# A hybrid decoder layer on Trainium2: 22,680 unread products of constants ahead of the first conditioning product

## The chip, the cores and the metric

The kernel runs on one core of one Trainium2 chip. The metric is the device time of one execution in microseconds, of the slowest (here the only) core. Times on TensorE, VectorE, ScalarE, GpSimd and SyncE are those of a hardware profile of one execution, in which these engines are called PE (with PEld for its weight loads), DVE, ACT, POOL and SP.

## What is computed

One layer of a decoder with 256 prompt tokens and 8 x 4 sample tokens (288 rows in all), model width 2,048. The conditioning product is the first matrix product; its results scale and shift everything that follows.

```python
def _layer(x, c, conv_prefix, chunk, g_mix, g_ffn, w_ada, b_ada, w_in, w_conv, g_v, w_sg, b_sg,
           w_pa, w_pb, w_out, w_ffn_in, w_ffn_out):
    n, s, _ = x.shape
    mod = (jax.nn.silu(c) @ w_ada + b_ada).reshape(n, N_MOD, 1, D_MODEL)
    sh_m, sc_m, gt_m, sh_f, sc_f, gt_f = [mod[:, i] for i in range(N_MOD)]
    h = _rms(x, g_mix) * (1 + sc_m) + sh_m
    proj = h @ w_in
    ...
    z = c_gate * hc
    conv = sum(w_conv[k] * zfull[:, k:k + s] for k in range(CONV_WIDTH))
    ya = b_gate * conv
    ...
    yb = u * sp.reshape(n, s, SG_DIM)
    merged = jax.nn.sigmoid(ga) * (ya @ w_pa) + jax.nn.sigmoid(gb) * (yb @ w_pb)
    x = x + gt_m * (merged @ w_out)
    h2 = _rms(x, g_ffn) * (1 + sc_f) + sh_f
    gate, up = jnp.split(h2 @ w_ffn_in, 2, axis=-1)
    x = x + gt_f * ((jax.nn.silu(gate) * up) @ w_ffn_out)
    ...
```

## The kernel before

All activations are held transposed, as 16 tiles of 128 features by 288 tokens. A weight matrix is streamed from HBM in blocks of at most 128 x 2,048 fp32 numbers into seven buffers (tag `raw`, `RAW = 7`). ScalarE casts 512 columns of a block to fp32r (`hi`, L448) and VectorE makes the rest (`lo`, L454, L243); the activations are split in the same way. A product of a 128x128 weight slice and a 128x288 activation tile is then a triple of three fp32r matmuls (L224, L227, L229): `hi` weight by `hi` activation, `hi` by `lo`, `lo` by `hi`. All weight slices start at a multiple of 128 elements in their buffer and all activation tiles at the start of theirs. In the first stages and in one later block the tile has ten columns more (`TU` = 298).

The conditioning product (class `Ada`, L388) is different: plain fp32, the 32 conditioning columns as the stationary operand, the weight block as the moving one, four 32-column strips at a time. Its units a0 and a1 (two blocks each) come first, and their results are needed for the first two tiles of the normalised input.

TensorE's instructions run in the order in which they are written. At the start that order is 24 bf16 matmuls of a tile of ones (`warm`, L571, into the PSUM tile `idle`), then a0's first block, five more such matmuls, a0's second block, and the first input tiles. For the start the orders of ScalarE, VectorE and SyncE are written by hand as well (a manual schedule that begins ahead of the first `load`). SyncE's queue issues the loads: a0, the first piece of w0, one x tile, the rest of w0, a1, another x tile, wK, wA and so on, each waiting until its buffer among the seven is free. The tile of ones `wb` is written by GpSimd.

The change touches only the function that writes this order (`_body`): it adds a nested function and one call of it, between the definitions and the list of steps, so its instructions stand ahead of the first `warm(24)` on TensorE.

```python
    wb = const("wb", [P, 288], BF16)
    G.memset(wb, 1.0)
    idle = psmain()
    ...
    steps = [Do(lambda: warm(24)), a0[0], Do(lambda: warm(5)), a0[1]]
    ...
    for s in stream[:2]:
        s.load()
    w0.load(0, 512)
    load_x(0)
    w0.load(512)
    for s in a1:
        s.load()
```

Of the kernel before, what the change touches and what calls it, by code (L numbers as in the profile page):

```python
# [8 lines left out]
F32 = mybir.dt.float32  # L9
F32R = mybir.dt.float32r  # L10
# [4 lines left out]
P = 128  # L15
D = 2048
T = 288
# [7 lines left out]
RAW = 7  # L25
# [59 lines left out]
def decoder_kernel(tc, d):  # L85
    nc = tc.nc
    from contextlib import ExitStack

    with ExitStack() as es:
        def pool(name, bufs=1, **kw):  # L90
            return es.enter_context(tc.tile_pool(name=name, bufs=bufs, **kw))

        pc = pool("const")
        pw = pool("wstream")
        pslot = pool("slots", SLOTS)
        ptmp = pool("tmp", 5)
        pps = pool("psum", 4, space=bass.MemoryType.PSUM)
        with tc.manual_schedule(engines={nc.tensor.engine}):
            _body(tc, nc, d, pc, pw, pslot, ptmp, pps)


def _body(tc, nc, d, pc, pw, pslot, ptmp, pps):
    ids = [0]

    def nm(s):
        ids[0] += 1
        return f"{s}_{ids[0]}"

    def const(name, shape, dt=F32):
        return pc.tile(shape, dt, tag=name, name=name)  # L110
# [7 lines left out]
    def psmain():  # L118
        return pps.tile([P, 512], F32, tag="main", name=nm("pm"), bufs=4)
# [4 lines left out]
    V, A, G, PE, SY = nc.vector, nc.scalar, nc.gpsimd, nc.tensor, nc.sync  # L124
# [227 lines left out]
    class Step:  # L352
        defer = False
        raw = None
# [209 lines left out]
# [3 lines that stand above are left out]
# [475 lines left out]
        tail.close()  # L1042


    rh1 = h1.__getitem__
    def at(main, plan):
        out, n = [], 0
        for s in main:
            out.append(s)
            if isinstance(s, Blk):  # L1050
                n += 1
                out += plan.pop(n, [])
        assert not plan
        return out
# [101 lines left out]
    for s in steps:  # L1156
# [11 lines left out]
        i = pos[id(s)]  # L1168
# [124 lines left out]
```

## Time and profile before

| | us |
|---|---|
| median of 2 runs (1624.91 to 1625.12) | 1625.01 |
| the profiled execution | 1625.02 |
| its span, first to last instruction | 1623.2 |
| TensorE busy with matmuls | 1613.2 |
| VectorE busy | 1015.8 |
| ScalarE busy | 736.2 |
| mean DMA rate over the span | 220 GB/s |

The time lies 1.8 us above the span: it holds what is around the first and the last instruction. Busy times add the durations of single instructions where they do not overlap; matmuls do overlap, so a matmul's own duration is longer than the distance to the next one's start. A row of the timeline shows start, duration, engine, line, operation, the tile written and the tiles read, and how many alike follow each other in it. In the table by windows the number in brackets counts the instructions that were active in the window.

In the first 40 us the DMA engines move some 400 GB/s, and the first conditioning product starts at 6.29 us.

### The profile page before, as it was taken

To read this page: it belongs to the slowest core of one execution; us is meant where nothing else is said; L and a number is where in the kernel's file an instruction comes from. 1 tells how busy PE (TensorE), PEld (TensorE's weight loads), DVE (VectorE), ACT (ScalarE), POOL (GpSimd) and SP (SyncE) were. 2 spreads that over 40 slices of the span, in tenths; PEclk is the share of its full clock that TensorE was granted. 3 is DMA by queue.
4 is the path that set the end of the run, shared out by engine and by line. 5 is a ranking of instruction groups with operands and counts; after the bars stand their busy time and mean duration, and the time that the engine had idled before them with its cause. 6 is when DMAs were issued, how large, how long until landed. Compare 5 with 4: busy or idle time off the path is not lost.

```text
span 1623.2 us, 31599 instructions
## 1 busy us (share of the span) xinstructions
PE 1613.2 (99%) x12645; PEld 1549.3 (95%) x12645; DVE 1015.8 (63%) x2196; ACT 736.2 (45%) x1358; POOL 21.8 (1%) x66
## 2 busy tenths in 40 slices
PE   9999999999999999999999999999999999999997
PEld 8998999999999999999999999999999999999997
DVE  6676788877755567667744555555555555555565
ACT  5533344643444334456633444444444444444454
POOL 0000000000000000011000000000000000000000
PEclk9999999999999999999999999999999999999999
DMA  9887866777877666654576556453464434645341
GB/s 376 324 318 286 313 238 212 273 284 289 298 292 309 261 260 228 241 178 158 185 307 263 207 180 209 156 173 110 164 229 157 168 121 161 225 157 172 110 161 59
DMA packets 59140, 357.60 MB, mean 220 GB/s; under 512 B 6736, under 2 KB 9840, under 8 KB 28272
## 3 DMA queue, kind: packets, MB, share of 16 engines
q1 hardware_dynamic: 58704, 355.45, 60.0%
q8 instruction: 99, 1.62, 0.4%
q14 instruction: 49, 0.40, 0.1%
q10 hardware_dynamic: 288, 0.13, 0.0%
HBM read 352.46 MB, written 3.09 MB: 219 GB/s over the span
## 4 chain that ended last, share of the span: by engine, by line
PE 98%; DMA 1%; DVE 0%; DVEq 0%; ACT 0%; issue 0%; ACTq 0%
PE pm L224 31%; PE pm L227 31%; PE pm L229 30%; PE ada L388 5%; DMA raw<-in_wK 1%; DMA raw<-in_w 0%; DVE st L1023 0%; DMA ct<-in_c 0%; PE px L227 0%; PE px L818 0%; PE px L224 0%; PE px L229 0%; PE px L859 0%; PE px L198 0%; PE px L860 0%; PE px L861 0%
## 5 line engine op out<-in xcount | busy, mean ns | idle before, releaser
L224 PE MATMUL pm<-s,hi 128*128 128x288 f32 (+1 forms) x3750 | 1108.9, 296 | 0.0
L227 PE MATMUL pm<-s,hi 128*128 128x288 f32 (+1 forms) x3750 | 1105.0, 295 | 0.0
L229 PE MATMUL pm<-s,lo 128*128 128x288 f32 (+1 forms) x3738 | 1101.3, 295 | 0.0
L448 ACT CAST hi<-raw 128x512 fp32r<-128x512 f32 (+1 forms) x963 | 587.4, 612 | 812.0 <-PE pm L227 776.7
L454 DVE TENSOR_TENSOR lo<-raw,hi 128x512 fp32r<-128x512 f32 (+1 forms) x849 | 577.2, 681 | 439.2 <-ACT hi L448 426.8
L224 PEld LDWEIGHTS pm<-s,hi 128*128 128x128 f32 x3750 | 705.1, 188 | 15.2 <-issue 13.3
L227 PEld LDWEIGHTS pm<-s,hi 128*128 128x128 f32 x3750 | 704.7, 188 | 0.0
L229 PEld LDWEIGHTS pm<-s,lo 128*128 128x128 f32 x3738 | 702.7, 188 | 0.0
L243 DVE TENSOR_TENSOR lo<-raw,hi 128x512 fp32r<-128x512 f32 x111 | 74.7, 676 | 29.6 <-ACT hi L448 28.9
L388 PE MATMUL ada<-raw,cs 128*32 128x512 f32 (+2 forms) x1152 | 88.3, 452 | 0.0
L388 PEld LDWEIGHTS ada<-raw,cs 128*32 128x32 f32 x1152 | 30.9, 110 | 44.7 <-issue 42.0
L766 DVE TENSOR_TENSOR s<-pm,s 128x288 f32<-128x288 f32 x72 | 32.9, 457 | 19.8 <-PE pm L229 19.8
L298 DVE TENSOR_TENSOR s<-t,s 128x288 fp32r<-128x288 f32 (+1 forms) x76 | 34.6, 459 | 6.4 <-ACT s L296 6.4
L296 ACT CAST s<-t 128x288 fp32r<-128x288 f32 (+1 forms) x76 | 32.5, 433 | 12.9 <-DVE t L798 12.4
L338 DVE SCALAR_TENSOR_TENSOR x<-pm,mod,x 128x256 f32<-128x256 f32 x79 | 37.5, 475 | 0.0
L944 DVE SCALAR_TENSOR_TENSOR t<-t,pm 128x288 f32<-128x288 f32 x42 | 19.1, 454 | 20.6 <-PE pm L229 20.6
L758 DVE TENSOR_TENSOR s<-pm,s 128x288 f32<-128x288 f32 x48 | 21.8, 454 | 10.4 <-PE pm L229 9.5
L337 DVE TENSOR_TENSOR t<-pm,mod 128x32 f32<-128x32 f32 x79 | 15.2, 192 | 18.5 <-PE pm L229 18.5
L743 DVE SCALAR_TENSOR_TENSOR s<-pm,s 128x256 f32<-128x256 f32 x48 | 23.1, 480 | 4.1 <-PE pm L229 4.1
L749 DVE TENSOR_TENSOR s<-s,rb 128x288 f32<-128x288 f32 x48 | 21.5, 449 | 0.0
L172 ACT ACTIVATE t<-x 128x288 f32<-128x288 f32 x29 | 12.9, 445 | 17.4 <-DVE x L341 17.4
L177 DVE TENSOR_TENSOR acc<-acc,t 128x288 f32<-128x288 f32 x33 | 15.0, 456 | 8.2 <-ACT t L172 8.2
(158 smaller groups left out, 479.7 us busy)
## 6 DMA issues: line engine op xcount, KB each, us to landing
raw<-in_fi SPq DMA_DIRECT2D x84, 1024.0 KB, 4.9
raw<-in_a SPq DMA_DIRECT2D x64, 1024.0 KB, 8.8
raw<-in_f SPq DMA_DIRECT2D x64, 704.0 KB, 4.0
raw<-in_wD SPq DMA_DIRECT2D x34, 1024.0 KB, 5.7
raw<-in_aE SPq DMA_DIRECT2D x16, 1024.0 KB, 10.3
raw<-in_wo SPq DMA_DIRECT2D x16, 1024.0 KB, 6.4
raw<-in_wC SPq DMA_DIRECT2D x19, 768.0 KB, 5.7
raw<-in_pa SPq DMA_DIRECT2D x8, 1024.0 KB, 5.9
```

Of the source, the lines that this page charges most:

```text
L224: PE.matmul(out, wh, ah, start=first, stop=False)
L227: end_ = PE.matmul(out, wh, al, start=False, stop=turn and last)
L229: end_ = PE.matmul(out, wl, ah, start=False, stop=last)
L243: lows.pop(0)[1]()
L296: A.copy(hi, a)
L298: V.tensor_tensor(lo, a, hi.bitcast(F32), ALU.subtract)
L338: V.scalar_tensor_tensor(x[:, m, :TP], ps[:, :TP], mod[:, gt0 + m, 0:1], x[:, m, :TP], ALU.mult, ALU.add)
L388: PE.matmul(acc[32 * j : 32 * j + 32, :w], cs[:, kt, :], self.raw[:, o : o + w], start=kt == 0, stop=kt == 15, tile_position=(0, 32 * j), ...
L448: A.copy(hi, self.raw[:, s * 128 : e * 128])
L454: sub()
L743: V.scalar_tensor_tensor(t[:, :TP], ps[:, :TP], t[:, T : T + 1], t[:, :TP], ALU.add, ALU.add)
L766: V.tensor_tensor(a, ps[:, :T], a, ALU.add)
```

## The change

A function `bench` is added and called once. VectorE fills a 128x2,048 tile with 0.75 and casts it to an fp32r tile; ScalarE casts it to two more. These four tiles take four of the seven stream buffers. TensorE runs 48 bf16 matmuls on `wb`, then walks a list of 1,260 combinations (s, a, b, l) of start places. For each of them it runs six triples: weight slices of the first tile start at i x 128 + s, moving operands of the third tile at s + a and 512 + s + b, and weight slices of the second tile at i x 128 + s + l, all in elements of four bytes. The first 320 entries have s = 0, five fixed values of a = b, and l from 0 to 63; the next 400 are drawn at random with a = b; the last 540 are drawn freely. All products go to the PSUM tile `idle`, each one with both start and stop set, and nothing reads it.

```diff
+    def bench():
+        import random
+
+        f = pw.tile([P, 2048], F32, tag="raw", name=nm("bench"), bufs=RAW)
+        V.memset(f, 0.75)
+        rs = []
+        for i in range(3):
+            r = pw.tile([P, 2048], F32R, tag="raw", name=nm("benchr"), bufs=RAW)
+            A.copy(r, f) if i else V.tensor_copy(r, f)
+            rs.append(r)
+        r0, r1, r2 = rs
+        def mm(s, m):
+            PE.matmul(idle[:, :T], s, m, start=True, stop=True)
+
+        def w(r, k, s=0):
+            return r[:, P * (k % 12) + s : P * (k % 12) + s + P]
+
+        def mv(r, o):
+            return r[:, o : o + T]
+
+        for i in range(48):
+            mm(wb[:, :P], wb)
+        rng = random.Random(2)
+        combos = [(0, a, a, b) for a in (7, 11, 23, 47, 63) for b in range(64)]
+        for i in range(400):
+            a = rng.randrange(64)
+            combos.append((rng.randrange(8), a, a, rng.randrange(64)))
+        for i in range(540):
+            combos.append((rng.randrange(8), rng.randrange(64), rng.randrange(64), rng.randrange(64)))
+        for s, a, b, l in combos:
+            for i in range(6):
+                mm(w(r0, i, s), mv(r2, s + a))
+                mm(w(r0, i, s), mv(r2, 512 + s + b))
+                mm(w(r1, i, s + l), mv(r2, s + a))
+
+    bench()
     rh1 = h1.__getitem__
```

Nothing of the old order is moved. On ScalarE two casts come between the activation of the conditioning vector and the first cast of a weight block; `bench` is the tile of 0.75 and `benchr` are fp32r tiles. In the changed kernel the rows are:

```order
L155 ACTIVATE ctt<-ct 128x144
L1053 CAST benchr_101<-bench_97 128x2048
L1053 CAST benchr_103<-bench_97 128x2048
L448 CAST hi_22981<-raw_22841 128x512
L677 ACTIVATE s_22986<-x,gm_89 128x256
```

Before, the cast of L448 stands right behind the activation of L155.

On SyncE's queue the loads keep their order, but not what they wait for. Before, the four pieces of a1 (`raw_111` and `raw_114`), the x tile behind them and wK wait for the DMA queues' own semaphores alone:

```order
L370 DMA raw_111<-in_a 128x1024 [waits DMAHW3_49]
L370 DMA raw_111<-in_a 128x1024 [waits DMAHW4_49]
L370 DMA raw_114<-in_a 128x1024 [waits DMAHW5_49]
L370 DMA raw_114<-in_a 128x1024 [waits DMAHW6_49]
L146 DMA x<-in_x 128x288 [waits DMAHW7_49]
L432 DMA raw_118<-in_wK 128x768 [waits DMAHW0_49]
```

In the changed kernel the same six rows are:

```order
L370 DMA raw_22847<-in_a 128x1024 [waits DMAHW3_49,DVE_49,Activation_49]
L370 DMA raw_22847<-in_a 128x1024 [waits DMAHW4_49]
L370 DMA raw_22850<-in_a 128x1024 [waits DMAHW5_49,PE_49]
L370 DMA raw_22850<-in_a 128x1024 [waits DMAHW6_49]
L146 DMA x<-in_x 128x288 [waits DMAHW7_49]
L432 DMA raw_22854<-in_wK 128x768 [waits DMAHW0_49,PE_49]
```

a1's first block now takes the buffer of the tile of 0.75 and waits for the casts that read it. Its second block and wK take buffers of constants that TensorE reads, and wait for TensorE; what stands behind them in the queue waits with them.

## The prediction

> **What bounds the kernel now.** I read the page's busy times first, then its chain of waits and its groups, then the table by windows for the pace of TensorE, and at last the timeline of the start, because the change is put there.
>
> ```profile
> span 1623.2 us, 31599 instructions
> ...
> PE 1613.2 (99%) x12645; PEld 1549.3 (95%) x12645; DVE 1015.8 (63%) x2196; ACT 736.2 (45%) x1358; POOL 21.8 (1%) x66
> ...
> PEclk9999999999999999999999999999999999999999
> ...
> PE 98%; DMA 1%; DVE 0%; DVEq 0%; ACT 0%; issue 0%; ACTq 0%
> ...
> L224 PE MATMUL pm<-s,hi 128*128 128x288 f32 (+1 forms) x3750 | 1108.9, 296 | 0.0
> L227 PE MATMUL pm<-s,hi 128*128 128x288 f32 (+1 forms) x3750 | 1105.0, 295 | 0.0
> L229 PE MATMUL pm<-s,lo 128*128 128x288 f32 (+1 forms) x3738 | 1101.3, 295 | 0.0
> ...
> L224 PEld LDWEIGHTS pm<-s,hi 128*128 128x128 f32 x3750 | 705.1, 188 | 15.2 <-issue 13.3
> ```
>
> TensorE is busy for 1613.2 of 1623.2 us, 98% of the chain that ended last is its own work, and the three matmul lines never idle ahead of themselves. So anything put in TensorE's queue and waited for by nobody still moves everything behind it. The mean of one (295 ns) is not its price: 11,238 of these at 295 ns would be 3.3 ms, twice the span. Matmuls overlap, and the price is the distance from start to start. That I read from a long window and from two rows of the timeline inside it.
>
> ```profile
> core 0: us, PE busy (x), PEclk, DMA share, GB/s
> 900.00:1600.00 700.00, 700.00 (x5297) 1.00 0.48 162
> ```
>
> ```profile
> 1199.72 0.30 PE L229 MATMUL pm<-s,lo 128*128 128x288 f32 x1
> ...
> 1201.98 0.30 PE L227 MATMUL pm<-s,hi 128*128 128x288 f32 x1
> ```
>
> In the window 5,297 matmuls are counted, of which about two had begun ahead of it (each lasts 0.30 us), so 700 / 5,295 = 132.2 ns each, at a granted clock of 1.00. The two timeline rows have 17 matmuls from the first's start to the second's: 2.26 / 17 = 132.9 ns. The long window averages more operands, so 132.2 ns is the pace I use. Nothing in TensorE idles in that window (700.00 of 700.00 us busy), so it is TensorE's own pace.
>
> **The change part by part.** The list of places has 320 + 400 + 540 = 1,260 entries; each is run over six weight slices with three matmuls each, so 1,260 x 6 x 3 = 22,680 fp32r matmuls of 128x288, and 48 bf16 ones ahead of them. Each group of three is the kernel's own triple: one weight with two moving operands, then a second weight with the first. Nothing is removed. All added matmuls write one PSUM tile that nobody reads, but TensorE works in order and the first conditioning product (L388) stands behind them.
>
> The start tells when they begin and what they displace.
>
> ```profile
> 0.83 0.17 DVE L149 MEMSET ones<- 128x128 f32 x1 [0.83 <-PEq L1272]
> ...
> 1.07 0.48 DVE L153 MEMSET cs<- 128x512 f32 x1
> ...
> 1.12 5.24 PE L571 MATMUL pm<-wb 128*128 128x288 bf16 x24 [1.12 <-POOL wb L565]
> ...
> 4.83 0.32 ACT L155 ACTIVATE ctt<-ct 128x144 f32<-128x144 f32 x1 [1.90 <-DMA ct<-in_c]
> ...
> 6.29 1.10 PE L388 MATMUL ada<-raw,cs 128*32 128x64 f32 x64
> ...
> 6.74 3.01 SPq L370 DMA_DIRECT2D raw<-in_a  x4
> ```
>
> ```profile
> L448 ACT CAST hi<-raw 128x512 fp32r<-128x512 f32 (+1 forms) x963 | 587.4, 612 | 812.0 <-PE pm L227 776.7
> ...
> L296 ACT CAST s<-t 128x288 fp32r<-128x288 f32 (+1 forms) x76 | 32.5, 433 | 12.9 <-DVE t L798 12.4
> ```
>
> ```profile
> 10.05 1.15 PE L571 MATMUL pm<-wb 128*128 128x288 bf16 x8
> ```
>
> *Begin.* Two chains must be done. The 48 bf16 matmuls start at 1.12 us as the 24 do now. The last of a row lasts about 0.29 us past its start, so the 24 of the slow start take (5.24 - 0.29) / 23 = 0.215 us each on average, and the eight at 10.05 us take (1.15 - 0.29) / 7 = 0.123 us. With 24 of the first and 24 of the second kind the 48 are issued by about 1.12 + 24 x 0.215 + 24 x 0.123 = 9.2 us. The other chain is the third constant tile, the later of two ScalarE casts of 128x2048 that stand behind the activation at 4.83 us. From 128x288 to 128x512 a cast grows by 179 ns per 224 elements, 0.80 ns each, so one of 2,048 elements is estimated at 0.612 + 1,536 x 0.80 = 1.84 us, and two end at 5.15 + 3.7 = 8.9 us. The fill on VectorE (from 0.17 us at 128 elements and 0.48 at 512, an estimated 1.7 us) is done by 3.4 us, ahead of both. So the 22,680 begin at about 9.2 us.
>
> *Their price.* No row of the trace has a TensorE operand that starts at an odd place: weight slices start at multiples of 128 elements and the moving tiles at the start of a buffer. The price lies between two neighbours. Below is the bf16 matmul of the same 288 columns, itself on constants, at 123 ns, the lowest pace that this trace has for so many columns. Above is the fp32r matmul of 298 columns:
>
> ```profile
> 768.88 0.30 PE L224 MATMUL pm<-s,hi 128*128 128x298 f32 x1
> ...
> 769.98 0.30 PE L229 MATMUL pm<-s,lo 128*128 128x298 f32 x1
> ```
>
> Eight of these take 1.10 us, 137.5 ns each. So the ends are 123 and 138 ns, 2,790 and 3,130 us in sum. I take 132.2 ns: same type, same columns, same order of weights, nearest in everything but the place. 22,680 x 132.2 ns = 2,998 us.
>
> *Behind them.* From the first conditioning product on, 1623.2 - 6.29 = 1616.9 us remain. Four of the seven buffers of the stream hold the constants, so SP stops at the second block of a1 until the matmuls are over, and wK, the next x tiles and wA queue behind it. I cost this at nothing, because SP gets no further now: it issues the blocks of a1 from 6.74 us on, 0.45 us behind the first conditioning product, and by then the changed kernel has a0, w0, the first x tile and half of a1 in place with the DMA queues empty. If that cover fails, the loss is one block's landing, some 7 us; the gain is bounded by TensorE's idle time now, 1623.2 - 1613.2 = 10 us. Both are under 0.3% of the sum. Fills and casts on VectorE and ScalarE lie beside the bf16 matmuls.
>
> *Sum.* 9.2 + 2,998 + 1,616.9 = 4,624 us of span. The profiled execution took 1625.02 us around its span of 1623.2, and the median of the runs is 1625.01, so 1.8 us are added: 4,626 us.
>
> A rule that speaks against this price: TensorE: Matmul & The Clock Gate of the Trainium skill, section Back-to-back issue gap, gives a warm gap of N/2.4 + 2.5 ns, 122.5 ns at N = 288; by it the added part would be 2,778 us and the sum 4,406 us. The trace agrees with it for bf16 (123 ns) and not for the fp32r triples (132.2 ns), so the row decides here.
>
> **The rivals.**
> 1. *Cheap places.* If the 9 ns between the two rows come from how the two operands' places fall together, scattered places can cost less: down to 123 ns, 22,680 x 123 = 2,790, in all 4,418 us. For it: the bf16 row. Against it: the pace hardly moves over 700 us in which the kernel goes through many buffers.
> 2. *Dear places.* An odd start can cost as an odd length does: ten more columns cost 5.3 ns (137.5 against 132.2) where 123/288 per column makes 4.3, so about 1 ns, 133.2 ns each and 4,649 us in all; the 298-column row itself caps it at 138 ns, 4,758 us. Against it: the same pace over 700 us, as above. SBUF — State Buffer of the Trainium skill, section Door 1, speaks of lines of 16 bytes and a penalty for each crossing; 288 fp32 columns from an odd start touch 73 such lines, not 72, which as an estimate is 134.0 ns and 4,667 us, and no run here shows an odd start.
> 3. *Weights no longer covered.* If a weight slice at an odd place can't be loaded beside the running matmul, its 188 ns become the pace: 4,264 us, in all 5,892 us. Against it: now 188 ns loads run at a 132 ns pace, so loads overlap each other.
> 4. *A slower clock.* At the pace of the start (215 ns) they would take 4,876 us, in all 6,504 us. Against it: the clock row is nines throughout, at 99% busy for 1.6 ms.
> 5. *Not slower.* The products are left out because nobody reads them: then the time stays 1,625 us. It decides only if the matmuls never reach TensorE; in its 10 us of idle time 22,680 would need 0.44 ns each, where the cheapest row has 123. Against it: the built program lists them all in TensorE's queue.
>
> **How the numbers follow.** The forecast, the pace of today's triples within 2.5 ns (129.7 to 134.7 ns, 4,570 to 4,683 us), gets 0.62; cheap places 0.14; dear places 0.16; uncovered weights 0.04; a slower clock 0.03; not slower 0.01. The time given is the likeliest, 4,626 us. The range takes in the forecast and nearly all of rivals 1 and 2, from 124 ns (4,440 us) to 138 ns (4,758 us), and leaves out the last three and the far ends, about 0.12. The change makes the kernel slower by over 2% (about what can be told from no change) in all cases but the fifth: 0.99 slower, 0.01 the same, and 0 faster.
>
> **What would show it.** The profile after should have some 22,700 more matmuls in one stretch from about 9 us to about 3,007 us with DMA near zero after its first microseconds, one window of 100 us in it counting about 759 matmuls at a clock of 1.00, the first conditioning product right behind, and from there the old 1,617 us. A count near 815 speaks for cheap places, near 725 for dear ones, near 530 for uncovered weights. Windows whose counts differ would show that places matter. The prediction is wrong if the pace is outside 124 to 138 ns, or if the stretch behind the first conditioning product is not within 10 us of 1,617.

## The result, and the profile after

| | before | after |
|---|---|---|
| median of 2 runs, us | 1625.01 | 4634.86 (4634.81 to 4634.91) |
| profiled span, us | 1623.2 | 4633.1 |
| ratio to before (95% interval) | | 2.8522 (2.8399 to 2.8645) |

The forecast was 4,626 us. These are the lines of the page after that answer to those shown of before: span, busy times, the chain by engine and by line, and the added groups.

```profile
span 4633.1 us, 77063 instructions
...
PE 4623.4 (100%) x35373; PEld 4558.6 (98%) x35373; DVE 1019.1 (22%) x2198; ACT 740.2 (16%) x1360; POOL 21.6 (0%) x66
...
PE 100%; DVE 0%; DVEq 0%; ACT 0%; issue 0%; POOL 0%; POOLq 0%
PE pm L1057 65%; PE pm L224 11%; PE pm L227 11%; PE pm L229 11%; PE ada L388 2%; PE pm L571 0%; DVE st L1023 0%; PE px L227 0%; PE px L224 0%; PE px L818 0%; PE px L229 0%; PE px L859 0%; PE px L198 0%; PE px L860 0%; PE pm L226 0%; PE px L861 0%
...
L1057 PE MATMUL pm<-benchr,benchr 128*128 128x288 f32 x22680 | 3006.7, 295 | 0.0
L1057 PEld LDWEIGHTS pm<-benchr,benchr 128*128 128x128 f32 x22680 | 3006.5, 188 | 0.0
L224 PE MATMUL pm<-s,hi 128*128 128x288 f32 (+1 forms) x3750 | 1108.3, 296 | 0.0
```

All 22,680 matmuls are there, in one stretch on the chain. Their own mean of 295 ns and that of the weight loads, 188 ns, are those of the kernel's triples; as before, neither is the price. The stretch's two ends stand in the timeline (start, duration, engine, line, operation):

```profile
1.12 7.80 PE L1057 MATMUL pm<-wb 128*128 128x288 bf16 x48 [1.12 <-POOL wb L565]
...
4.67 3.68 ACT L1053 CAST benchr<-bench 128x2048 fp32r<-128x2048 f32 x2
...
8.67 3.52 PE L1057 MATMUL pm<-benchr,benchr 128*128 128x288 f32 x25
```

```profile
3015.25 3.11 PE L571 MATMUL pm<-wb 128*128 128x288 bf16 x24
3018.29 1.10 PE L388 MATMUL ada<-raw,cs 128*32 128x64 f32 x64
```

From 8.67 to 3015.25 us are 3,006.58 us, 132.57 ns for each of 22,680. Then come the kernel's own 24 bf16 matmuls, 3.04 us, and 4633.1 - 3018.29 = 1,614.8 us from the first conditioning product to the end, 2.1 us less than before (1,616.9).

The mean hides three parts. The table by windows, cut at the borders of the list (320, 400 and 540 combinations):

```profile
core 0: us, PE busy (x) PEld busy (x) DVE busy (x) ACT busy (x) POOL busy (x), PEclk, DMA share, GB/s
10.00:760.00 750.00, 750.00 (x5751) 750.00 (x5750) 0.00 (x0) 0.35 (x1) 0.00 (x0) 1.00 0.01 3
762.00:1718.00 956.00, 956.00 (x7181) 956.00 (x7180) 0.00 (x0) 0.00 (x0) 0.00 (x0) 1.00 0.00 1
1721.00:3014.00 1293.00, 1293.00 (x9698) 1293.00 (x9697) 0.00 (x0) 0.00 (x0) 0.00 (x0) 1.00 0.00 1
```

With the two matmuls that had begun ahead of each window left out, that is 130.5, 133.2 and 133.4 ns. TensorE is alone, at a clock of 1.00, with VectorE and ScalarE idle, and still the pace differs. So the places matter: the first part's five moving starts (7, 11, 23, 47, 63) are all 3 modulo 4. Sorting the 400 combinations with a = b by (s + a) modulo 4, from the starts of their first matmuls in the trace, gives 132.35, 135.23, 133.98 and 131.14 ns for 0, 1, 2 and 3. Sorted by the place of the third matmul's weights they hardly differ (132.97 to 133.63 ns by s + l modulo 4).

### The profile page after: what moved, and what is told of

It reads as the page before. It is cut to its first block, busy times and chain, and to the rows that moved or that the text cites. A ratio compares the mean times of both kernels' runs of the same rounds, so it can differ in the third digit from the quotient of the medians.

```text
span 4633.1 us, 77063 instructions
## 1 busy us (share of the span) xinstructions
PE 4623.4 (100%) x35373; PEld 4558.6 (98%) x35373; DVE 1019.1 (22%) x2198; ACT 740.2 (16%) x1360; POOL 21.6 (0%) x66
## 4 chain that ended last, share of the span: by engine, by line
PE 100%; DVE 0%; DVEq 0%; ACT 0%; issue 0%; POOL 0%; POOLq 0%
PE pm L1057 65%; PE pm L224 11%; PE pm L227 11%; PE pm L229 11%; PE ada L388 2%; PE pm L571 0%; DVE st L1023 0%; PE px L227 0%; PE px L224 0%; PE px L818 0%; PE px L229 0%; PE px L859 0%; PE px L198 0%; PE px L860 0%; PE pm L226 0%; PE px L861 0%
## 5 line engine op out<-in xcount | busy, mean ns | idle before, releaser
L1057 PE MATMUL pm<-benchr,benchr 128*128 128x288 f32 x22680 | 3006.7, 295 | 0.0
L1057 PEld LDWEIGHTS pm<-benchr,benchr 128*128 128x128 f32 x22680 | 3006.5, 188 | 0.0
L224 PEld LDWEIGHTS pm<-s,hi 128*128 128x128 f32 x3750 | 704.9, 188 | 15.2 <-issue 13.3
L448 ACT CAST hi<-raw 128x512 fp32r<-128x512 f32 (+1 forms) x963 | 587.7, 612 | 803.6 <-PE pm L227 778.6
```

Source lines behind the costliest of these rows:

```text
L224: PE.matmul(out, wh, ah, start=first, stop=False)
L448: A.copy(hi, self.raw[:, s * 128 : e * 128])
L1057: PE.matmul(idle[:, :T], s, m, start=True, stop=True)
```

## Experiments

All comparisons are with the kernel before, run on the same chip beside them. The theories: **P**, the place of a moving operand's first element modulo four elements (16 bytes) sets the pace; against it **T** (drift with time), **W** (the weights' places), **V** (the values), **K** (other waits hide it in the real kernel).

### One class of moving starts at a time: start0, start1, start2, start3

The weights keep their drawn places; of the moving starts all have one remainder C.

```diff
-                mm(w(r0, i, s), mv(r2, s + a))
-                mm(w(r0, i, s), mv(r2, 512 + s + b))
-                mm(w(r1, i, s + l), mv(r2, s + a))
+                mm(w(r0, i, s), mv(r2, (s + a) // 4 * 4 + C))
+                mm(w(r0, i, s), mv(r2, 512 + (s + b) // 4 * 4 + C))
+                mm(w(r1, i, s + l), mv(r2, (s + a) // 4 * 4 + C))
```

start0:

> The list of 1,260 combinations, but every moving operand's start rounded down to a multiple of four elements (0 modulo 4); weights stay at their drawn places. Theory P (the place of the moving operand's start modulo four elements, 16 bytes, sets the pace): the second part of the list in the changed kernel has 132.35 ns for such starts, so 1,628.1 us outside the stretch + 22,680 x 132.35 ns = 4,630 us. Theory T (the pace drifts with time in the run, first fast, then slow): all four variants 4,635 us. Theory W (the weights' drawn places set it): all four 4,635 us.

start1:

> As start0, but all moving starts 1 modulo 4. Theory P: 135.23 ns each, 4,695 us. Theories T and W: 4,635 us, with the windows of the first 750 us at 768 matmuls per 100 us under T.

start2:

> As start0, but all moving starts 2 modulo 4. Theory P: 133.98 ns each, 4,667 us. Theories T and W: 4,635 us.

start3:

> As start0, but all moving starts 3 modulo 4. Theory P: 131.14 ns each, 4,602 us. Theories T and W: 4,635 us.

| | expected by P, us | measured, us | ratio to before (95% interval) | ns each |
|---|---|---|---|---|
| start0 | 4,630 | 4629.60 | 2.8492 (2.8450 to 2.8535) | 132.3 |
| start1 | 4,695 | 4700.27 | 2.8923 (2.8879 to 2.8966) | 135.4 |
| start2 | 4,667 | 4669.98 | 2.8736 (2.8688 to 2.8784) | 134.1 |
| start3 | 4,602 | 4598.67 | 2.8297 (2.8255 to 2.8339) | 131.0 |

The last column is the time less the 1,628.3 us that the changed kernel has outside its stretch (4634.86 - 3,006.58), by 22,680. T and W wanted 4,635 us four times; both fall. One window each, the same for all (start0, start1, start2, start3 in this order; us, PE busy and matmuls, clock, DMA):

```profile
1000.00:2900.00 1900.00, 1900.00 (x14353) 1.00 0.00 1
```

```profile
1000.00:2900.00 1900.00, 1900.00 (x14034) 1.00 0.00 1
```

```profile
1000.00:2900.00 1900.00, 1900.00 (x14160) 1.00 0.00 1
```

```profile
1000.00:2900.00 1900.00, 1900.00 (x14489) 1.00 0.00 1
```

TensorE is 100% busy in each and the clock is the same; only the count of matmuls that fit differs, by 3.2% from the dearest to the cheapest class. That is the count to look at, since neither the busy time nor the mean of one shows it.

### The weights' places: weights_even

```diff
-                mm(w(r0, i, s), mv(r2, s + a))
-                mm(w(r0, i, s), mv(r2, 512 + s + b))
-                mm(w(r1, i, s + l), mv(r2, s + a))
+                mm(w(r0, i), mv(r2, s + a))
+                mm(w(r0, i), mv(r2, 512 + s + b))
+                mm(w(r1, i), mv(r2, s + a))
```

> The changed kernel with all weight slices at multiples of 128 elements (s and l left out of their starts), moving operands as drawn. Theory P (moving starts alone set the pace): 4,635 us within 5. Theory W (odd weight starts cost something of their own, which the drawn weights of the four runs before hide alike): at least 10 us less, under 4,625 us.

Measured: 4631.83 us, ratio 2.8501 (2.8458 to 2.8545). In its trace the stretch runs at 132.43 ns, 0.14 ns under the 132.57 of the changed kernel. Odd weight places cost next to nothing.

### The values: drawn_data

```diff
-        V.memset(f, 0.75)
+        SY.dma_start(f, d["fi"][0])
```

> The changed kernel with the constant tiles filled from the first block of the FFN weights (1 MB from HBM) in place of 0.75. Theory P (values don't matter): the pace of the changed kernel, 132.57 ns, and a start some 4 to 6 us later, because the casts wait for the load: 4,639 to 4,641 us, granted clock 1.00. Theory V (constants flatter the price): a granted clock under 1.00 or windows of 100 us with under 745 matmuls, 4,670 us or more.

Measured: 4636.03 us, ratio 2.8528 (2.8489 to 2.8567). The stretch begins at 10.09 us in place of 8.67 (the load was quicker than I took it to be) and runs at 132.57 ns, as with constants. V falls: the values don't move the pace on this one core.

### The fixed part, and the gain behind the stretch: short and later

```diff
-        for s, a, b, l in combos:
+        for s, a, b, l in combos[:2]:
```

> The changed kernel with the first 2 combinations alone, 36 fp32r matmuls and the 48 bf16 ones. Fixed part: 1,625.0 + (8.67 - 6.29) for the later start + 2.95 for the kernel's own 24 bf16 matmuls, which stood beside the first load before + 36 x 0.131 = 1,635.0 us. Theory L (the 2.1 us that the changed kernel gains behind its first conditioning product come from loads that had 3 ms to land): little of it here, 1,634 to 1,635 us. Theory B (they come from the order or the buffers, whatever the stretch's length): 1,632.9 us.

Measured: 1633.72 us, ratio 1.0052 (1.0039 to 1.0064), between the two. The trace parts it: the first conditioning product starts at 17.19 us (16.3 were expected; the fp32r matmuls begin at 9.36 us in place of 8.67), and 1,615.0 us remain behind it, 1.9 less than before. So the gain needs no 3 ms. Whether it comes from the head start of the loads or from the buffers and the order that the constants bring, was asked without the constants:

```diff
-    steps = [Do(lambda: warm(24)), a0[0], Do(lambda: warm(5)), a0[1]]
+    steps = [Do(lambda: warm(104)), a0[0], Do(lambda: warm(5)), a0[1]]
```

> The kernel before with 104 bf16 matmuls on ones in place of 24 ahead of the first conditioning product, 80 x 0.1225 = 9.8 us more; buffers and load order as before. Theory H (the 2 us gained behind the first conditioning product come from the head start of the loads on TensorE): 1,616.9 us behind it become some 1,615.0, in all 1,632.9 us. Theory B (they come from the buffers and the order that the four constant tiles bring): 1,616.9 us behind it, in all 1,634.8 us.

Measured: 1632.09 us, ratio 1.0044 (1.0031 to 1.0056). Timeline of SyncE and TensorE at its start:

```profile
6.74 2.92 SPq L370 DMA_DIRECT2D raw<-in_a  x4
```

```profile
15.58 0.63 PE L388 MATMUL ada<-raw,cs 128*32 128x64 f32 x29
```

The loads of a1 are issued at 6.74 us as before, but the first conditioning product starts at 15.58 us, and from there 1,614.6 us remain, 2.3 less than before. So some nine microseconds ahead of the first conditioning product, without any tile of constants, give the same 2 us as the change does: the constants aren't needed for it. (80 bf16 matmuls more moved the first conditioning product by 9.3 us, not 9.8.)

H is not shown by that. In the first 16 us from the first conditioning product on 0.7 us are gained; there a wait of TensorE for VectorE, 0.34 us at 21.69 us in the kernel before, shrinks to 0.03 us. For most of the other 1.6 us the trace shows no wait: the same matmuls run a little faster. These are 120 us from the same place on, 150 us behind the first conditioning product, in the kernel before and in later (us, PE busy and matmuls, clock, DMA):

```profile
156.29:276.29 120.00, 120.00 (x916) 1.00 0.70 257
```

```profile
165.58:285.58 120.00, 120.00 (x922) 1.00 0.71 259
```

Six matmuls more fit. From start to start, none of them differs by more than 40 ns between the two runs, and their small differences add up to 1.0 us, in later, in short and in the changed kernel alike. Nor are the buffers of later those of before, as its expectation has it: in the programs as built, later, short and the changed kernel all put 216 of the 11,328 fp32r moving tiles into other slots than the kernel before, the same slots in all three. Head start and slots changed together, so which of them gives these 1.6 us stays open.

### What is paid once and what per column: lengths

In place of the list, 240 matmuls each at 12 lengths and three starts, in one execution.

```diff
-        for s, a, b, l in combos:
...
+        for c in (0, 1, 3):
+            for n in (64, 128, 192, 256, 284, 286, 288, 290, 292, 298, 384, 512):
+                for i in range(240):
+                    PE.matmul(idle[:, :n], w(r0, i % 6), r2[:, 64 * (i % 5) + c : 64 * (i % 5) + c + n], start=True, stop=True)
```

> In place of the list: 240 fp32r matmuls each of 64 to 512 moving columns, at starts 0, 1 and 3 modulo 4, weights at multiples of 128. Theory F (what an fp32r matmul costs above bf16, some 10 ns at 288 columns, and what the start adds, 4.1 ns between starts 1 and 3, is paid once per matmul): 512 columns take about 227 ns, and starts 1 and 3 differ by 4 ns at 128 and at 512 columns alike. Theory C (it is paid per column): 512 columns take about 235 ns, and starts 1 and 3 differ by 2 ns at 128 and by 7 at 512.

In the table by windows the rows are 128 columns at start 0; 288 and 512 at start 0; 288 and 512 at start 1; 288 and 512 at start 3 (us, PE busy and matmuls, clock, DMA):

```profile
62.00:106.00 44.00, 44.00 (x209) 0.50 0.00 1
232.00:260.00 28.00, 28.00 (x214) 1.00 0.00 1
404.00:454.00 50.00, 50.00 (x222) 1.00 0.00 1
680.00:707.00 27.00, 27.00 (x201) 1.00 0.00 1
854.00:905.00 51.00, 51.00 (x218) 1.00 0.00 0
1126.00:1154.00 28.00, 28.00 (x215) 1.00 0.00 1
1297.00:1347.00 50.00, 50.00 (x220) 1.00 0.00 1
```

And 290 columns at starts 0, 1 and 3:

```profile
262.00:293.00 31.00, 31.00 (x235) 1.00 0.00 1
709.00:740.00 31.00, 31.00 (x235) 1.00 0.00 1
1156.00:1187.00 31.00, 31.00 (x235) 1.00 0.00 1
```

From the distances of their starts, 288 columns take 131.7, 135.5 and 131.1 ns at starts 0, 1 and 3, and 512 columns take 226.7, 236.7 and 228.9 ns. At start 0, 256, 384 and 512 columns take 120.0, 173.3 and 226.7 ns: 53.3 ns for each 128 columns more, and 13.3 ns that do not grow. So something is paid once per matmul, as F has it. That the 9 ns between fp32r and bf16 are paid once is not shown, since bf16 ran at 288 columns alone; and lengths near 288 leave that line by some nanoseconds (133.3 ns at 284, 128.9 at 286).

What start 1 costs above start 3 fits neither F nor C: 6.7 ns at 256 columns, 4.4 at 288, 5.0 at 384 and 7.8 at 512, but nothing at 290, where all three starts take 133.3 ns. The order of the starts that was found at 288 columns therefore can't be carried to another length untried.

At 128 columns nothing can be told of the starts: the granted clock is 0.50 there, and all three take 213.3 ns. So do 64 columns at that clock, and the first of 192; at 1.00, 64 and 192 columns both take 111.7 ns. Between 64 and 192 columns it is thus not their number that sets the pace. Whether the weight load ahead of each matmul does was not tested.

### Into the kernel: slots1, slots3, slots7

The kernel before, without the added products. Only the place of the activation tiles in their slots changes. The slots are no larger: in the programs as built they lie 1,216 bytes (304 elements) apart in all four kernels, and every moving operand's tile keeps its slot.

```diff
-        return pslot.tile(list(shape), dt, tag="s", name=nm("s"), padded_shape=[P, TU])
+        p, n = shape
+        t = pslot.tile([p, n + 3], dt, tag="s", name=nm("s"), padded_shape=[P, TU + 3])
+        return t[:, 3 : 3 + n]
```

For slots1 the 3 is a 1; for slots7 it is 7 where n is 288 or less and 3 otherwise, with 304 as the padded length.

slots1:

> The kernel before, without the added products; every activation tile starts one element behind the start of its slot, so that the moving operands of the 11,316 triple matmuls start at 1 modulo 4. Theory P (the start's place costs in the kernel what it costs in the stretch of constants): 135.2 - 132.3 = 2.9 ns each, 33 us more, 1,658 us. Theory K (in the kernel other waits hide it): 1,625 us within 5.

slots3:

> As slots1, but three elements behind the start of the slot (start 3 modulo 4). Theory P: 131.1 to 131.5 ns, 0.8 to 1.2 ns less each, 9 to 14 us less, 1,611 to 1,616 us. Theory K: 1,625 us; a third outcome, over 1,630 us, would say that VectorE or ScalarE, which write the same tiles, pay for the odd start.

slots7:

> As slots3, but tiles of 288 columns start seven elements behind the start of the slot (3 modulo 4 and 7 modulo 8), tiles of 298 columns three. Theory P: 130.8 ns, 1.4 ns less for some 10,900 matmuls, 15 us less, 1,610 us. Theory K: 1,625 us.

| | expected by P, us | measured, us | ratio to before (95% interval) | ns per triple matmul of 288 columns |
|---|---|---|---|---|
| before | | 1624.96 | 1 | 132.17 |
| slots1 | 1,658 | 1662.85 | 1.0232 (1.0218 to 1.0246) | 135.64 |
| slots3 | 1,611 to 1,616 | 1611.69 | 0.9918 (0.9904 to 0.9931) | 130.97 |
| slots7 | 1,610 | 1619.52 | 0.9966 (0.9952 to 0.9980) | 131.71 |

The last column is the mean distance from a triple matmul's start to the next one's in the trace, over some 10,800 distances under 150 ns (about 40 longer ones are left out). A window of 600 us late in the kernel shows it as a count, for before, slots1 and slots3 in this order:

```profile
900.00:1500.00 600.00, 600.00 (x4541) 1.00 0.50 169
```

```profile
900.00:1500.00 600.00, 600.00 (x4432) 1.00 0.49 171
```

```profile
900.00:1500.00 600.00, 600.00 (x4590) 1.00 0.49 168
```

K falls: the kernel pays for the place of its moving operands in full, 10,800 x (132.17 - 130.97) = 13.0 of the 13.3 us that slots3 gains. slots3 is faster than the kernel before by 0.8%, which is under 2%, but the interval of the ratio lies clear of 1. slots7 is a miss. In the stretch of constants starts of 7 modulo 8 took 130.8 ns and those of 3 modulo 8 took 131.5; in the kernel it is 131.71 against 130.97, the other way round. What sets the fine part within a class isn't settled by these runs. That there is more to it than the class shows in the kernel before too: as built, all its triples' moving tiles start at the same place modulo 64 bytes, and still the mean runs from 129.6 to 135.1 ns from slot to slot (slots with 100 such matmuls or more).

## Why the prediction was right

**Begin of the stretch.** 9.2 us were given, 8.67 measured. The casts took 3.68 us for two, as worked out (3.7); the slow start of the bf16 matmuls ended earlier, after 15 of them at some 240 ns, at 4.7 us; in the kernel before it took 18, to 5.4 us.

**Price.** 132.2 ns were given, 132.57 measured: 8.3 us over 22,680. The step was to take the kernel's own triple, nearest in everything but the place, for a place that no row showed. It held, but not because places cost nothing. Rivals 1 and 2, cheap and dear places, both happened, in different parts of the list: 130.5 ns in the first 320 combinations, 133.2 and 133.4 in the rest. Had the list been all of start 1 it would have been 4,700 us, all of start 3 4,599 us; the mean over the list lies near the kernel's own class, start 0 (132.35 ns), because its first part happens to be all of the cheapest class. That the total came so close is luck of this list. The argument against both rivals, that the pace hardly moves over 700 us of the kernel, was weak: all its moving operands start in one class, so it showed no other. The 1 ns that rival 2 took from the ten longer columns has the right size for the drawn starts (133.4) and the wrong rule. SBUF — State Buffer of the Trainium skill, section Door 1, makes every crossing into a new 16-byte line cost something. Starts 1, 2 and 3 all touch 73 lines where start 0 touches 72, yet 1 and 2 cost more than 0, and 3 costs less (start1, start2, start3 against start0), so the measurement decides against a plain count of lines.

**A step left out.** The sum went from the end of the stretch straight to the first conditioning product. The kernel's own 24 bf16 matmuls stand between them; in the old timeline they lay ahead of 6.29 us and so outside the 1,616.9 us. They cost 3.04 us.

**Behind the first conditioning product.** I costed the held-back loads at nothing, with a bound of 10 us for a gain. It was a gain of 2.1 us. In later, without the constants, it is there too; 0.6 us of it fall in the first 16 us, where TensorE waits less, and most of the rest is a slightly faster pace of the same matmuls, whose cause is open. The bound was drawn from TensorE's idle time, and a faster pace lies outside that reasoning. SP's wait itself is in the trace: in the changed kernel a1's second block waits 3,006 us for TensorE and is issued at 3015.30 us, 3 us ahead of the first conditioning product, where before a1 was issued behind it.

**The sum.** -0.5 + 8.3 + 3.0 - 2.1 = 8.7 us, which is the difference of 4634.86 and 4626.2 us. The omission and the gain nearly cancel; the rest is the pace.

**The other rivals.** Uncovered weights (5,892 us): loads of 188 ns stay covered at odd places, 132.43 against 132.57 ns in weights_even. A slower clock (6,504 us): 1.00 in every window of the stretch, with drawn data as well. Left out: all 22,680 are in the trace.

## What to carry to other kernels

Price a matmul by the distance of starts in a window that TensorE fills, never by its own duration, and count from the trace what else stands between the cut and the row that you continue from. Where TensorE is the bound, the first element of the moving operand within its 16 bytes is worth a try: with 288 columns, moving it from 0 to 3 modulo four fp32 elements gave 0.8% here at no cost in memory, and 1 modulo four lost 2.3%. Try it at your own length: at 290 columns starts 0, 1 and 3 cost the same. A mean over drawn cases can sit near one known case by cancellation, so look at the parts before calling the step confirmed.

## What the hardware showed that I had not expected

- For fp32r matmuls of 288 columns the moving operand's start modulo 16 bytes moves the mean pace: 132.3, 135.4, 134.1 and 131.0 ns for 0, 4, 8 and 12 bytes. At 290 columns 0, 4 and 12 bytes all took 133.3 ns. The weights' start does not (0.14 ns). Why 12 bytes is cheapest is open.
- At 128 moving columns with a weight load each, the granted clock was 0.50 and a matmul took 213 ns, where one of 192 columns right behind took 111.7 ns once the clock was back at 1.00. TensorE was 100% busy by the profile in both. TensorE: Matmul & The Clock Gate of the Trainium skill, Part 1, has the two states 4/8 and 8/8, set by how busy the array was; the 0.50 agrees with that, and a busy time of 100% here was not enough to hold the full clock.
